# Down projection of a SwiGLU block as seven block products instead of eight, on one Trainium2 core

## The chip, the cores and the metric

The kernel runs on one core of a Trainium2 chip. The metric is the device time of one execution in microseconds (us). TensorE (PE in the profile, its weight loads PEld) multiplies matrices, VectorE (DVE), ScalarE (ACT) and GpSimd (POOL) do elementwise work, SyncE (SP) issues most of the DMAs.

## The reference

A trunk of two layers on 1024 tokens of width 1024 in float32: an mLSTM mixer, then chunked attention, each followed by a SwiGLU feed-forward block with hidden width 2816, and a final RMSNorm. What the change touches:

```python
def swiglu(h, w_gate, w_up, w_down):
    return (jax.nn.silu(h @ w_gate) * (h @ w_up)) @ w_down

# per layer
h = h + swiglu(rmsnorm(h, norm_ffn_g[l]), ffn_w_gate[l], ffn_w_up[l], ffn_w_down[l])
# after the last layer
return rmsnorm(h, final_norm_g)
```

## The kernel before

Everything is kept transposed: features on the 128 partitions, tokens along the row. A feature tile is 128 features by 1024 tokens (a half: 512 tokens), so the residual `h` is 8 tiles and the hidden layer 22. For float32 accuracy each operand is split into a rounded part and a remainder (`split_into`: ScalarE copies the rounded part, VectorE subtracts), and each block of a product takes three matmuls: high by high, low by high, high by low.

The gate and up projections (`gate_up`) already work by 2x2 blocks in seven products, as in the method of Strassen and Winograd. Feature tiles p and p+11 and the two token halves make the blocks. A unit is one pair of tiles of one of the two matrices; there are 22 units, worked one after the other, and each has products c = 0 to 6 of 12 matmuls of 512 columns. `prepare` makes the seven weight sums of a unit and their splits (`wc`), seven products ahead. The operand sums come from `Mixed`: `mix` makes those of products 0 to 3 while the mixer's output projection is running, `late` those of products 4 to 6 (`b21`, `t4`, `b22`), which the first unit calls for between its own products. `st.finish` turns the sums of squares into the norm's factors `f_rbc` after product 3 of the first unit. `add` also stores `h` to DRAM (`hd`). `gate` and `up` finish each half tile, and `up` stores the hidden tile to DRAM (`hid`).

The down projection (`ffn`) multiplies the plain way. The 22 hidden tiles are cut into four blocks of 4, 6, 6 and 6 tiles (`PBLOCKS`). For each block `fetch` loads the hidden tiles and splits them, and for each of the 8 output tiles and both halves the block's matmuls run (tile `d_p`) and VectorE adds the result to `h` (L1073). Weights come through `Weights`, one tile ahead. In layer 0 the last block also makes the statistics and the operands of attention (`finalize_mid`), in layer 1 it works by columns 0 to 511, 512 to 767 and 768 to 1023 (`PIECES`, tile `dl`), and normalises, scales and stores each piece as soon as it is whole (`finalize_last`).

Instructions are traced in the order of the code; a scheduler then sets each engine's queue, and an instruction may go ahead of earlier ones when its data and its buffers are free. A tile waits until the tiles that lay in its memory have been used for the last time. The pool `core` has 25 tiles of 128 x 1024; in `gate_up` 24 of them hold the operand sums.

Of the kernel before, what the change touches and what calls it, by code (L numbers as in the profile page):

```python
# [8 lines left out]
F32 = mybir.dt.float32  # L9
F32R = mybir.dt.float32r  # L10
# [7 lines left out]
NK = 8  # L18
# [7 lines left out]
PBLOCKS = (2, 3, 3, 3)  # L26
# [7 lines left out]
PIECES = ((0, 512), (512, 256), (768, 256))  # L34
# [7 lines left out]
def tile_trunk(  # L42
# [80 lines left out]
    class Weights:  # L123
# [9 lines left out]
        def add(self, key, src, n=T, g=None, pool=None):  # L133
            self.specs.append((key, src if isinstance(src, list) else [src], n, g, pool))
# [52 lines left out]

    def feat_cols(w, xs, ps, cols):

        whi, wlo = w  # L190
        n = len(xs)
        for k in range(n):
            wh = whi[:, k * P : (k + 1) * P]
            wl = wlo[:, k * P : (k + 1) * P]
            xh, xl = (a[:, cols] for a in xs[k])
            for i, (a, b) in enumerate(((wh, xh), (wl, xh), (wh, xl))):
                nc.tensor.matmul(  # L197
                    ps, a, b, start=(k == 0 and i == 0), stop=(k == n - 1 and i == 2)
                )
            yield 3  # L200
# [16 lines left out]
    def tok_proj(wv, xs, name, evac):  # L217

        for c in range(T // P):
            pv = pjt(f"{name}_{c}")  # L220
            for k in range(NK):
                wh, wl = (w[:, (k % 4) * 256 : (k % 4 + 1) * 256] for w in wv[k // 4])
                xh, xl = (a[:, c * P : (c + 1) * P] for a in xs[k])
                for i, (a, w) in enumerate(((xh, wh), (xh, wl), (xl, wh))):
                    nc.tensor.matmul(  # L225
                        pv[:, 0:256], a, w, start=(k == 0 and i == 0), stop=(k == 7 and i == 2)
                    )
                if k % 2:
                    yield 3
            evac(c, pv)  # L230
# [118 lines left out]
    def down_weights(layer):  # L349
        p0 = 0  # L350
        for b, nb in enumerate(PBLOCKS):
            last = layer == 1 and b == len(PBLOCKS) - 1
            for e in range(NK):
                src = [
                    w_down[layer, e][:, (p0 + d) * P : (p0 + d + nb) * P] for d in (0, NP)
                ]
                wts.add(("d", layer, b, e), src, 2 * nb * P, pool="core" if last else None)
            p0 += nb

    wts.fence()  # L360
    down_weights(0)
# [10 lines left out]
    wts.fence()  # L372
    down_weights(1)
# [467 lines left out]
    class Mixed:  # L841
# [60 lines left out]
    def gate_up(layer, mixed, st):  # L902
# [24 lines left out]
        def prepare(m):  # L927

            n, c = divmod(m, NC)
# [16 lines left out]
            t = full("hl", f"wc{layer}{m}", F32R)  # L946
# [3 lines left out]
            ready[m] = t  # L950

        at = [0]

        def product(n, c, ps, name, first):
            m = n * NC + c
            ahead = AHEAD if n else min(AHEAD, 2 + c)
            while at[0] < min(m + 1 + ahead, NC * len(units)):
                prepare(at[0])
                at[0] += 1
            w = ready.pop(m)  # L960
# [26 lines left out]

        def up(f, h, x, ps=None):
# [5 lines left out]
            if f not in hid:  # L994
                hid[f] = dram.tile([P, T], F32, tag=f"f{layer}{f}", name=f"hid{layer}{f}")
            nc.sync.dma_start(hid[f][:, hs(h)], x)

        for n, (p, i) in enumerate(units):
# [10 lines left out]
            if n == 0:  # L1009
                mixed.late(0)  # L1010
                mixed.late(1)
# [4 lines left out]
            if n == 0:  # L1016
                mixed.late(2)
                mixed.late(3)
# [3 lines left out]
            tt(c22, c, v, ALU.add)  # L1022
            d = pjt(f"d{layer}{n}")
# [4 lines left out]
            done(p + NP, 1, c22)  # L1028
            product(n, 4, a, "b21", False)
            done(p, 0, tmp("c11"), a)  # L1030
            product(n, 5, c, "t4", False)
            c21 = tmp("c21")
            tt(c21, c, v, ALU.add)
            done(p + NP, 0, c21)
            product(n, 6, d, "b22", False)
            tt(v, v, d, ALU.subtract)
            done(p, 1, v)
        sb.close()
# [3 lines left out]
    def ffn(layer, mixed, st, finalize):  # L1042
        psc = Scope(mx=2, pj=6)
        kept = gate_up(layer, mixed, st)
        wsc = wscope()
        sb = Scope(half=6, hr=2, ex=16)
        pairs = iter(range(NP))
        blocks = []
        for nb in PBLOCKS:
            ps_ = [next(pairs) for _ in range(nb)]  # L1050
            blocks.append(ps_ + [p + NP for p in ps_])

        def fetch(b, f):
            raw = full("hr" if b else "core", f"hr{layer}{f}")
            nc.sync.dma_start(raw, kept[f])
            return split(raw, f"hid{layer}{f}", pool="ex" if b % 2 else "core")

        hid = [fetch(0, f) for f in blocks[0]]
# [5 lines left out]
        for b, fs in enumerate(blocks):  # L1064
            if b == len(blocks) - 1:
                finalize(layer, b, h, hid)
                break
            nxt = []
            for e in range(NK):

                def ed(hh, ps):
                    s_ = h[e][:, hs(hh)]
                    nc.vector.tensor_tensor(s_, s_, ps, ALU.add)  # L1073

                run(feat(wts.get("d", layer, b, e), hid, f"d{layer}{b}{e}", ed))
                if len(nxt) < len(blocks[b + 1]):
                    nxt.append(fetch(b + 1, blocks[b + 1][len(nxt)]))
            hid = nxt
        psc.close()
        sb.close()  # L1080
        return wsc

    def finalize_mid(layer, b, h, hid):
        st = Stats("b")
        for e in range(NK):

            def ed(hh, ps):
                s_ = h[e][:, hs(hh)]
                nc.vector.tensor_tensor(s_, s_, ps, ALU.add)
                st.add(s_, hs(hh))  # L1090

            run(feat(wts.get("d", layer, b, e), hid, f"d{layer}{b}{e}", ed))
            xb.append(split(h[e], f"xb{e}"))
        stb.append(st)

    def finalize_last(layer, b, h, hid):
        st = Stats("fin")
        ws = [wts.get("d", layer, b, e) for e in range(NK)]
        r_bc = ext("fin_rbc")
        for c0, n in PIECES:  # L1100
            cols = slice(c0, c0 + n)
            for e in range(NK):
                ps = pjt(f"dl{c0}_{e}")[:, 0:n]
                run(feat_cols(ws[e], hid, ps, cols))
                s_ = h[e][:, cols]
                nc.vector.tensor_tensor(s_, s_, ps, ALU.add)
                st.add(s_, cols)
            st.finish(r_bc, cols)
            for e in range(NK):
                s_ = h[e][:, cols]  # L1110
                if e % 3 == 0:
                    nc.scalar.activation(s_, s_, AF.Copy, scale=gcol(G_FIN, e))
                    nc.gpsimd.tensor_tensor(s_, s_, r_bc[:, cols], ALU.mult)
                else:
                    nc.vector.scalar_tensor_tensor(
                        s_, s_, gcol(G_FIN, e), r_bc[:, cols], ALU.mult, ALU.mult
                    )
                (nc.sync if e % 2 else nc.scalar).dma_start(out[e][:, cols], s_)
# [235 lines left out]
    xb, stb = [], []  # L1354
    mixed, st = mlstm()
    wsc = ffn(0, mixed, st, finalize_mid)
    mixed, st = attention(xb, stb[0])
    wsc.close()
    ffn(1, mixed, st, finalize_last).close()
# [92 lines left out]
```

## Time and profile before

| | |
|---|---|
| Median of 3 runs | 2458.86 us (2457.55 to 2460.49) |
| Profiled execution, its own time | 2460.18 us |
| Its span | 2458.4 us |
| PE busy | 2383.3 us, 97% of the span |
| Mean granted TensorE clock | 0.989 of full |

A busy share says how long an engine had an instruction in work; overlapping instructions count once. Waits are put down to what came last before the waiting instruction started. The profiled execution is one run: 1.3 us above the median.

### The profile page before, as it was taken

Reading aid. Unit: us, or ns where it says so; the run is one execution under the profiler, and the core shown is the slowest. Engines: PE = TensorE matmul, PEld = TensorE weight load, DVE = VectorE, ACT = ScalarE, POOL = GpSimd, SP = SyncE. Lnnn points to the kernel's source line nnn. Section 1 sums busy time; section 2 is a strip of 40 time slices with the busy share of each in tenths; the row PEclk is TensorE's granted clock in tenths of the full one; section 3 lists DMA queues with packets and bytes.
Section 4 is the critical chain, followed back from the end, with each engine's and each line's share of the span. In section 5 each row is a group of like instructions: output and inputs, shape, how many; then the busy total and the mean of one; then the engine's idle time right before and its main releaser. Section 6 shows DMA issues by size and latency. Waiting matters only on the chain.

```text
span 2458.4 us, 31074 instructions
## 1 busy us (share of the span) xinstructions
PE 2383.3 (97%) x11844; PEld 1973.6 (80%) x11844; DVE 1508.8 (61%) x2451; ACT 890.7 (36%) x1592; POOL 887.3 (36%) x582
## 2 busy tenths in 40 slices
PE   8999999889999999999999999989899999999998
PEld 7888787768888888888879788878678888888887
DVE  6544446886666655334377777787976666645334
ACT  5322222543232333113366666655532233323122
POOL 2000000476455540003564545350865655530003
PEclk9999999989999999999999999999999999999999
DMA  3110102312222217211111111001222222145211
GB/s 134 44 35 26 43 29 75 134 68 82 94 85 80 83 59 261 88 60 52 49 44 44 37 37 41 30 23 48 107 78 103 78 78 86 69 160 192 62 58 69
DMA packets 74885, 185.85 MB, mean 76 GB/s; under 512 B 8304, under 2 KB 26992, under 8 KB 74736
## 3 DMA queue, kind: packets, MB, share of 16 engines
q1 hardware_dynamic: 73008, 181.76, 21.9%
q8 instruction: 93, 1.52, 0.3%
q10 hardware_dynamic: 1728, 2.10, 0.2%
q14 instruction: 56, 0.46, 0.1%
HBM read 148.18 MB, written 35.65 MB: 75 GB/s over the span
## 4 chain that ended last, share of the span: by engine, by line
PE 87%; DVE 7%; ACT 3%; issue 1%; POOL 1%; DMA 0%; SPq 0%; DVEq 0%; ACTq 0%; POOLq 0%
PE d_p L197 17%; PE d L966 10%; PE c L966 9%; PE a L966 9%; PE b L966 5%; PE pv L225 4%; PE ao_p L197 4%; PE pvb L225 4%; PE bq_p L197 2%; PE bk_p L197 2%; PE dl L197 2%; PE wa_p L197 2%; PE wb_p L197 2%; PE ak_p L197 2%; PE ob_p L197 2%; PE po L1272 2%
## 5 line engine op out<-in xcount | busy, mean ns | idle before, releaser
L966 PE MATMUL a<-b,wc 128*128 128x512 f32 x1056 | 265.9, 400 | 21.9 <-ACT wc L947 11.0
L966 PEld LDWEIGHTS a<-b,wc 128*128 128x128 f32 x1056 | 202.5, 193 | 70.1 <-ACT wc L947 11.8
L966 PE MATMUL c<-t,wc 128*128 128x512 f32 x1056 | 258.1, 394 | 0.0
L966 PEld LDWEIGHTS c<-t,wc 128*128 128x128 f32 x1056 | 199.9, 189 | 44.1 <-ACT wc L947 0.3
L949 DVE TENSOR_TENSOR wc<-s,wc 128x512 fp32r<-128x512 f32 x168 | 158.3, 944 | 94.2 <-ACT wc L947 92.3
L947 ACT CAST wc<-s 128x512 fp32r<-128x512 f32 x176 | 108.2, 619 | 216.7 <-PE d L966 127.9
L1073 DVE TENSOR_TENSOR hr<-hr,d_p 128x512 f32<-128x512 f32 x96 | 65.8, 686 | 162.1 <-PE d_p L197 161.9
L727 POOL TENSOR_TENSOR hv<-num 128x1024 f32<-128x1024 f32 x8 | 15.2, 1895 | 342.5 <-ACT num L703 342.5
L161 ACT CAST wh_d<-wr_d 128x768 fp32r<-128x768 f32 (+1 forms) x64 | 49.8, 781 | 241.2 <-PE d_p L197 223.8
L981 POOL TENSOR_TENSOR c<-c,f_rbc 128x512 f32<-128x512 f32 x44 | 75.1, 1707 | 157.4 <-DVE c L1027 150.0
L966 PE MATMUL d<-b,wc 128*128 128x512 f32 x528 | 131.1, 397 | 0.8 <-DVE c L1027 0.8
L966 PE MATMUL b<-t,wc 128*128 128x512 f32 x528 | 128.7, 393 | 3.0 <-POOL wc L949 1.8
L947 ACT CAST wc<-wr 128x512 fp32r<-128x512 f32 x132 | 81.1, 618 | 135.3 <-PE a L966 42.3
L966 PE MATMUL d<-n,wc 128*128 128x512 f32 x528 | 128.0, 391 | 0.0
L966 PEld LDWEIGHTS b<-t,wc 128*128 128x128 f32 x528 | 99.3, 188 | 25.7 <-POOL wc L949 2.5
L966 PEld LDWEIGHTS d<-b,wc 128*128 128x128 f32 x528 | 99.3, 188 | 25.2 <-DVE c L1027 1.2
L1232 ACT ACTIVATE p<-p,mn 128x640 f32<-128x640 f32 (+4 forms) x128 | 89.2, 697 | 83.6 <-DVE mn L1221 77.0
L966 PEld LDWEIGHTS d<-n,wc 128*128 128x128 f32 x528 | 99.2, 188 | 21.7
L991 POOL TENSOR_TENSOR c<-c,c 128x512 f32<-128x512 f32 x44 | 74.3, 1689 | 106.2 <-issue 69.2
L1236 DVE TENSOR_SCALAR p<-p,rs 128x640 f32<-128x640 f32 (+4 forms) x128 | 109.1, 852 | 2.9
L949 DVE TENSOR_TENSOR wc<-wr,wc 128x512 fp32r<-128x512 f32 x126 | 106.2, 843 | 6.1 <-ACT wc L947 5.7
L985 POOL TENSOR_TENSOR c<-c,f_rbc 128x512 f32<-128x512 f32 x66 | 94.5, 1434 | 30.3 <-ACT c L984 28.8
(1146 smaller groups left out, 6561.0 us busy)
## 6 DMA issues: line engine op xcount, KB each, us to landing
wr<-in_w_gate_dram SPq DMA_DIRECT2D x44, 512.0 KB, 4.3
wr<-in_w_up_dram SPq DMA_DIRECT2D x44, 512.0 KB, 4.3
hr<-hid SPq DMA_DIRECT2D x44, 512.0 KB, 3.7
wr_d<-in_w_down_dram SPq DMA_DIRECT2D x96, 192.0 KB, 2.5
hid<-c SPq DMA_DIRECT2D x66, 256.0 KB, 2.4
hd<-h SPq DMA_DIRECT2D x16, 512.0 KB, 2.7
hr<-hd SPq DMA_DIRECT2D x16, 512.0 KB, 6.0
hid<-v SPq DMA_DIRECT2D x22, 256.0 KB, 2.0
```

What stands on the lines that cost most here:

```text
L161: nc.scalar.copy(hi[:, :n], raw[:, :n])
L197: nc.tensor.matmul(ps, a, b, start=(k == 0 and i == 0), stop=(k == n - 1 and i == 2))
L225: nc.tensor.matmul(pv[:, 0:256], a, w, start=(k == 0 and i == 0), stop=(k == 7 and i == 2))
L947: nc.scalar.copy(t[:, 0:HT], src)
L949: eng.tensor_tensor(t[:, HT:T], src, t[:, 0:HT], ALU.subtract)
L966: nc.tensor.matmul(ps, a, b, start=(first and k == 0 and i == 0), stop=(k == len(xs) - 1 and i == 2), skip_group_check=True,)
L981: nc.gpsimd.tensor_tensor(x, x, r, ALU.mult)
L985: nc.gpsimd.tensor_tensor(x, x, r, ALU.mult)
L991: nc.gpsimd.tensor_tensor(x, x, g, ALU.mult)
L1073: nc.vector.tensor_tensor(s_, s_, ps, ALU.add)
L1232: nc.scalar.activation(p, p, AF.Exp, bias=mnv, scale=-1.0, accum_out=sm)
L1236: eng.tensor_scalar(p, p, rs, None, ALU.mult)
```

## The change

The down projection of both layers is done by 2x2 blocks in seven products as well: output tiles u and u+4, hidden tiles p and p+11, and the two token halves. Product by product, for each u = 0 to 3, one PSUM bank sums 11 feature tiles x 3 matmuls. `up` now makes the operand sums `n1`, `t2`, `t3`, `t4` per pair and stores seven half tiles instead of two whole ones. `fetch` brings one product's 11 half tiles into `core`; `combine` makes the weight sums in place in the raw weights; `settle` adds each product into the residual. In `gate_up` the first two units are interleaved: products 0 to 3 of both, then 4 to 6 of both, with one `late` after each of the first four products. Half of the stores of `h` move from `add` to `late`. The first weights of attention are no longer behind the down weights in one list, and matmuls with 8 operands take tiles 4 to 7 first in layer 1. The last norm is done by two halves. The core of the diff:

```diff
-PBLOCKS = (2, 3, 3, 3)
+WC = NP * P
-PIECES = ((0, 512), (512, 256), (768, 256))
-        def add(self, e, h):
+        def keep(self, e, h):
             kept = dram.tile([P, T], F32, tag=f"h{self.layer}{e}", name=f"hd{self.layer}{e}")
             nc.sync.dma_start(kept, h)
             self.kept[e] = kept
+        def add(self, e, h):
+            if e < NK // 2:
+                self.keep(e, h)
...
         def late(self, k):
             h2, t2 = self.got.pop(k)
             e = k + NK // 2
+            self.keep(e, h2)
...
+        order = [(n, c) for cs in (range(4), range(4, NC)) for n in range(2) for c in cs]
+        order += [(n, c) for n in range(2, len(units)) for c in range(NC)]
...
+            i, p = divmod(f, NP)
+            part[i, h] = x
+            if (i, h) != (0, 1):
+                store(f"b{i + 1}{h + 1}", p, x)
+                return
+            n1, t2, t3, t4 = (halft(f"{nm}{layer}_{p}") for nm in ("n1", "t2", "t3", "t4"))
+            nc.gpsimd.tensor_tensor(t3, part[1, 1], x, ALU.subtract)
+            store("t3", p, t3)
+            nc.vector.tensor_tensor(n1, part[0, 0], x, ALU.subtract)
+            store("n1", p, n1)
+            nc.vector.tensor_tensor(t2, part[1, 1], n1, ALU.add)
+            store("t2", p, t2)
+            nc.gpsimd.tensor_tensor(t4, part[1, 0], t2, ALU.subtract)
+            store("t4", p, t4)
...
+        first, second = unit(0), unit(1)
+        for k in range(4):
+            next(first)
+            mixed.late(k)
+        for _ in range(4):
+            next(second)
+        for u in (first, second):
+            for _ in u:
+                pass
...
+    def down(layer, mixed, hid):
+        sb = Scope(hr=6, half=8, wc=2, wd=12)
+        names = ("b11", "t2", "n1", "t4", "t3", "b21", "b22")
+        NU = NK // 2
+        pieces = [(c, min(HT, WC - c)) for c in range(0, WC, HT)]
...
+        def fetch(i, k):
+            r = hrt(f"hr{layer}{i}_{k}")
+            nc.sync.dma_start(r, hid[names[i], k])
+            t = coret(f"hc{layer}{i}_{k}", F32R)
+            split_into(t[:, 0:HT], t[:, HT:T], r)
+            sums[i, k] = t
+        def combine(i, u):
+            a11, a21, a22 = raw[u, 0, 0], raw[u, 1, 0], raw[u, 1, 1]
+            if i == 1:
+                nc.gpsimd.tensor_tensor(a21, a11, a21, ALU.subtract)
+                nc.vector.tensor_tensor(a21, a22, a21, ALU.subtract)
+            if i == 2:
+                nc.gpsimd.tensor_tensor(a11, a21, a11, ALU.add)
+            if i == 4:
+                nc.vector.tensor_tensor(a22, a22, a21, ALU.subtract)
+            if i == 6:
+                a12 = raw[u, 0, 1]
+                nc.gpsimd.tensor_tensor(a12, a21, a12, ALU.subtract)
+        def prepare(i, u):
+            t = pools["wc"].tile([P, 2, WC], F32R, tag="wc", name=f"wc{layer}{i}{u}")
...
+                split_into(t[:, 0, c : c + n], t[:, 1, c : c + n], src)
+            if i == 2:
+                wload(u, 0, 1)
...
+        def settle(i, u, ps):
...
+            if i == 0:
+                v[u] = halft(f"v{layer}{u}")
+                nc.scalar.copy(v[u], ps)
+                tt(r11, r11, ps, ALU.add)
+            if i == 1:
+                tt(v[u], v[u], ps, ALU.add)
+                for r in (r12, r21, r22):
+                    nc.gpsimd.tensor_tensor(r, r, v[u], ALU.add)
+            if i == 2:
+                tt(r22, r22, ps, ALU.subtract)
+                tt(r12, r12, ps, ALU.subtract)
+            if i in (3, 4):
+                tt(r21, r21, ps, ALU.add)
...
+        prepare(0, 0)
+        for k in range(NP):
+            fetch(0, k)
+        for u in range(NU):
+            wload(u, 0, 0)
         for e in range(NK):
             ht = coret(f"hr{layer}_{e}")
             nc.sync.dma_start(ht, mixed.kept[e])
             h.append(ht)
+        for u in range(NU):
+            wload(u, 1, 0)
+            wload(u, 1, 1)
+        order = [(i, u) for i in range(len(names)) for u in range(NU)]
+        for m, (i, u) in enumerate(order):
+            if m + 2 < len(order):
+                combine(*order[m + 2])
+            if m + 1 < len(order):
+                prepare(*order[m + 1])
+            w = wcs.pop((i, u))
+            ps = pjt(f"dn{layer}{i}{u}")
+            for k in range(NP):
+                wh, wl = (w[:, j, k * P : (k + 1) * P] for j in range(2))
+                x = sums[i, k]
+                xh, xl = x[:, 0:HT], x[:, HT:T]
+                for j, (a, b) in enumerate(((wh, xh), (wl, xh), (wh, xl))):
+                    nc.tensor.matmul(
+                        ps, a, b, start=(k == 0 and j == 0), stop=(k == NP - 1 and j == 2)
+                    )
+            if i + 1 < len(names):
+                for k in (range(0, 2), range(2, 4), range(4, 5), range(5, NP))[u]:
+                    fetch(i + 1, k)
+            settle(i, u, ps)
+            if last and i >= 5 and u == NU - 1:
+                if i == 5:
+                    r_fin.append(coret("fin_rbc"))
+                scale_out(i - 5)
```

## Rows read from the trace of the kernel before

**Rows 1.** Page, busy time of each engine, and the chain that ended last.
```profile
PE 2383.3 (97%) x11844; PEld 1973.6 (80%) x11844; DVE 1508.8 (61%) x2451; ACT 890.7 (36%) x1592; POOL 887.3 (36%) x582
PE 87%; DVE 7%; ACT 3%; issue 1%; POOL 1%; DMA 0%; SPq 0%; DVEq 0%; ACTq 0%; POOLq 0%
```
**Rows 2.** Busy time by stretch (start:end, length, then as the header says).
```profile
core 0: us, PE busy (x) PEld busy (x) DVE busy (x) ACT busy (x) POOL busy (x), PEclk, DMA share, GB/s
532.00:917.00 385.00, 385.00 (x1678) 314.96 (x1677) 249.90 (x297) 118.13 (x203) 220.78 (x143) 1.00 0.23 80
...
934.00:990.00 56.00, 56.00 (x247) 46.03 (x246) 32.97 (x40) 20.01 (x23) 1.49 (x2) 1.00 0.79 269
```
**Rows 3.** Chain in order of time, down projections (start us, us, what).
```profile
933.86 240.54 PE d_p L197 x1056
...
2199.05 175.20 PE d_p L197 x768
2374.25 33.60 PE dl L197 x144
...
2432.51 13.09 PE dl L197 x111
```
**Rows 4.** Timeline of PE, first units of gate and up, layer 0, then layer 1.
```profile
490.90 0.80 PE L966 MATMUL a<-b,wc 128*128 128x512 f32 x1 [6.36 <-ACT wc L947]
506.24 1.84 PE L309 MATMUL f_ps<-ones,f_s 128*128 128x1 f32 x16
513.37 0.50 PE L966 MATMUL a<-b,wc 128*128 128x512 f32 x1 [3.34 <-DVE b L179]
516.46 1.97 PE L966 MATMUL a<-b,wc 128*128 128x512 f32 x3 [2.59 <-ACT b L178]
531.16 2.91 PE L966 MATMUL b<-t,wc 128*128 128x512 f32 x12
...
1770.94 1.84 PE L309 MATMUL f_ps<-ones,f_s 128*128 128x1 f32 x16
1791.47 3.41 PE L321 MATMUL f_pb<-packed,f_y 128*128 128x128 f32 x16 [2.40 <-DVE f_y L278]
1796.36 2.91 PE L966 MATMUL b<-t,wc 128*128 128x512 f32 x12
```
**Rows 5.** Timeline of DVE in the same stretch of layer 0.
```profile
499.67 3.50 DVE L895 SCALAR_TENSOR_TENSOR t<-h,packed,t 128x512 f32<-128x512 f32 x2
...
516.18 1.40 DVE L179 SCALAR_TENSOR_TENSOR b<-h,packed,b 128x512 fp32r<-128x512 f32 x2
```
**Rows 6.** Durations by line: min/median/max ns, first and last start.
```profile
L949 DVE TENSOR_TENSOR wc<-s,wc x168: 675/694/1787, 517.5 to 2172.2; 128x512 fp32r<-128x512 f32 x168
L949 POOL TENSOR_TENSOR wc<-s,wc x8: 1280/1734/1754, 496.7 to 1776.5; 128x512 fp32r<-128x512 f32 x8
L163 POOL TENSOR_TENSOR wl_bq<-wr_bq,wh_bq x8: 2365/2388/2411, 1167.5 to 1569.7; 128x1024 fp32r<-128x1024 f32 x8
L176 DVE TENSOR_TENSOR hid01l<-hr,hid01h x1: 1225/1225/1225, 921.3 to 921.3; 128x1024 fp32r<-128x1024 f32 x1
L1073 DVE TENSOR_TENSOR hr<-hr,d_p x96: 678/687/690, 936.7 to 2374.3; 128x512 f32<-128x512 f32 x96
```
**Rows 7.** Busy time by stretch around the first down projection's start.
```profile
925.00:935.00 10.00, 10.00 (x45) 8.17 (x44) 4.93 (x6) 2.10 (x2) 2.88 (x3) 1.00 0.62 199
935.00:945.00 10.00, 10.00 (x46) 8.20 (x45) 2.87 (x5) 0.69 (x2) 1.01 (x1) 1.00 0.97 376
```
**Rows 8.** DMA issues: count, KB each, median us to landing.
```profile
hid<-c SPq DMA_DIRECT2D x66, 256.0 KB, 2.4
hr<-hd SPq DMA_DIRECT2D x16, 512.0 KB, 6.0
```
**Rows 9.** Chain at the end, after the first piece of 512 columns.
```profile
2414.00 1.11 PE fin_pb L321 x8
...
2415.76 6.59 DVE hr L1115 x5
```

More of the change, by code (lines that the diff above doesn't have):

```diff
@@ L185, in split, with k_order @@
         return hi, lo
+    second_first = [False]
+    def k_order(n):
+        if second_first[0] and n == NK:
+            return list(range(NK // 2, NK)) + list(range(NK // 2))
+        return list(range(n))
     def feat_cols(w, xs, ps, cols):
@@ L191, in feat_cols @@
         n = len(xs)
-        for k in range(n):
+        for at, k in enumerate(k_order(n)):
             wh = whi[:, k * P : (k + 1) * P]
@@ L197, in feat_cols @@
                 nc.tensor.matmul(
-                    ps, a, b, start=(k == 0 and i == 0), stop=(k == n - 1 and i == 2)
+                    ps, a, b, start=(at == 0 and i == 0), stop=(at == n - 1 and i == 2)
                 )
@@ L220, in tok_proj @@
             pv = pjt(f"{name}_{c}")
-            for k in range(NK):
+            for at, k in enumerate(k_order(NK)):
                 wh, wl = (w[:, (k % 4) * 256 : (k % 4 + 1) * 256] for w in wv[k // 4])
@@ L225, in tok_proj @@
                     nc.tensor.matmul(
-                        pv[:, 0:256], a, w, start=(k == 0 and i == 0), stop=(k == 7 and i == 2)
+                        pv[:, 0:256], a, w, start=(at == 0 and i == 0), stop=(at == 7 and i == 2)
                     )
@@ L347, in tile_trunk @@
         wts.add(("wb", e), w_aout[e][:, KA * P : T], T - KA * P)
[L349 to L358, printed above, removed]
     wts.fence()
-    down_weights(0)
     for t in range(8):
@@ L945, in prepare @@
             src = (a11, s2, s3, s1, a12, a22, s4)[c]
-            t = full("hl", f"wc{layer}{m}", F32R)
+            t = full("hl", f"wc{layer}{n}_{c}", F32R)
             nc.scalar.copy(t[:, 0:HT], src)
@@ L986, in gate, with store @@
             gs[f, h] = x
+        def store(name, p, x):
+            t = dram.tile([P, HT], F32, tag=f"{name}_{layer}{p}", name=f"k{name}_{layer}{p}")
+            nc.sync.dma_start(t, x)
+            hid[name, p] = t
+        part = {}
         def up(f, h, x, ps=None):
@@ L993, in up, with unit @@
                 nc.vector.tensor_tensor(x, ps, g, ALU.mult)
[L994 to L998, printed above, removed]
+            i, p = divmod(f, NP)
[12 more added lines that the diff above has]
+            store("t4", p, t4)
+        def unit(n):
+            p, i = units[n]
             done = (gate, up)[i]
@@ L1037, in gate_up @@
             done(p, 1, v)
+            yield
+        first, second = unit(0), unit(1)
[7 more added lines that the diff above has]
+                pass
+        for n in range(2, len(units)):
+            for _ in unit(n):
+                pass
         sb.close()
@@ L1063, in ffn @@
             h.append(ht)
[L1064 to L1078, printed above, removed]
@@ L1079, in ffn @@
-        psc.close()
[L1080 to L1118, printed above, removed]
@@ L1121, in attention, with ffn @@
+        sb.close()
+        return xs, st
+    def ffn(layer, mixed, st):
+        psc = Scope(mx=1, pj=7)
+        kept = gate_up(layer, mixed, st)
+        psc.close()
+        psc = Scope(mx=2, pj=6)
+        res = down(layer, mixed, kept)
+        psc.close()
+        return res
     def attention(xs, st):
@@ L1352, in attention @@
         return mixed, st
[L1354 removed]
     mixed, st = mlstm()
[L1356 to L1357 removed]
+    xb, st = ffn(0, mixed, st)
+    wsc = wscope()
+    second_first[0] = True
+    mixed, st = attention(xb, st)
     wsc.close()
[L1359 removed]
+    ffn(1, mixed, st)
     base.close()
```

99 lines of the change are left out of this document (70 added, 29 removed).

## Prediction

> **What bounds the kernel now.** I read the page first: TensorE is busy 97% of the span, and the chain that ended last runs 87% over it [rows 1]. That is a share of a whole; what a stage is worth has to be read in the stage. So next the busy times by stretch: in the steady part of gate and up, and in the first 56 us of the down projection, TensorE has no idle time at the full granted clock, VectorE is at 65% and 59% [rows 2]. The chain in order of time says the same: 1056 matmuls of the down projection in layer 0 follow one another in 240.54 us [rows 3], so one costs 240.54 / 1056 = 0.2278 us there. In these stages a matmul less is 0.2278 us less, as long as what feeds it keeps up. Last I read the two places where TensorE does stand: the first units of gate and up in both layers [rows 4] and the tail, 2458.4 - 2445.6 = 12.8 us after the last matmul (2432.51 + 13.09) [rows 3].
>
> **Matmuls.** Before: 8 output tiles x 2 halves x 22 hidden tiles x 3 = 1056 per layer. After: 7 products x 4 x 11 x 3 = 924, of the same shape and with a new weight for each, as before. Two layers: 264 x 0.2278 = -60.1 us.
>
> **The end of layer 1.** Before, from the first to the last matmul 2445.60 - 2199.05 = 246.5 us for work that at 0.2278 us takes 240.5: 6 us went to statistics and to waits between the three pieces. After there is one such break (4 row sums, then `fin_pb` of 1.11 us [rows 9]) in product 6: -3, between 0 and -5. The tail, however, now handles 512 columns instead of 256. Five scalings of 512 columns took 6.59 us [rows 9], so half of that, 3.3, is added there, and about 1.7 in the add, the square, the sum and a larger last store: +5, between 3.3 and 12.8 (all of it doubled). Together +2.
>
> **First units interleaved.** Layer 0: from the end of product 3 (506.24) to the second product of unit 1 (531.16) [rows 4] are 24.9 us, for four products of 12 x 0.2278 = 2.73 us, 1.84 us of row sums and, I take it, as much for the factors' matmuls `f_pb`: some 10.3 us are lost. Waits of 3.34 and 2.59 us for `late`'s splits are in it. Layer 1: 1770.94 to 1796.36 are 25.4 us, with 3.41 for `f_pb` some 9.2 are lost. The reason is VectorE, which works on `late` from 499.67 to 517.58 [rows 5]. Interleaved, four products of unit 1 (11 us) go in front of the first that needs `late`. But they want three more weight splits early (at up to 1.79 us each [rows 6], some 5 us), so VectorE ends `late` near 523 instead of 517.6, while TensorE asks at 506.24 + 1.84 + 11 = 519. I take 6 of 10 us as won, in two layers -12; the bounds are 0 (unit 1's weights late instead) and -20 (all of it). The wait of 6.36 us ahead of the first product stays: nothing there is taken away but stores of `h` that move behind it, which I count at nothing.
>
> **Start of the down projection.** Until product 1 starts, 4 x 33 x 0.2278 = 30.1 us in, these must land: 11 half tiles (2.9 MB), the first weights twice for one tile and once for three (3.6 MB), `h` (4.2 MB), the other eight weight halves (5.8 MB), five half tiles of product 1 (1.3 MB): 17.7 MB. The DMAs moved 199 GB/s in the 10 us around the boundary and 376 when 97% busy [rows 7]. 30.1 us at 376 are 11.3 MB; the other 6.4 MB have to come in the 20 us before, in which the weight tiles and the operands of products 0 to 2 of the last unit fall free. At 199 that is 4.0 MB, 2.4 short, 6.4 us late; at 376 nothing is late. I take +3 per layer, bounds 0 and 6.4.
>
> **The port of VectorE and GpSimd.** A subtraction of 512 columns with both inputs in SBUF takes VectorE 0.69 us, but up to 1.79; GpSimd takes 1.28 alone and 1.73 in the median [rows 6]. Additions that read PSUM keep to 0.68 to 0.69 throughout. So the first kind hardly overlaps with GpSimd: 0.69 + 1.28 = 1.97 us of work in 1.79. By columns, a weight half of 1408 takes VectorE 1.225 x 1.375 = 1.7 us and GpSimd 2.39 x 1.375 = 3.3 us. In products 1 and 2 (60.2 us) GpSimd has 6 combines (19.7) and 12 additions of `settle` (15.4); VectorE has 2 combines (3.4), 8 weight splits (8 x 2.75 x 0.694 = 15.3) and 22 operand splits (15.3). That is 69 us one after the other, or 63 at the overlap seen; 12 additions from PSUM (8.3) also stand in VectorE's queue. The 12 GpSimd additions may slip into product 3, where GpSimd has no other work, so the loss can be nothing; at most it is 69.1 + 8.3 - 60.2 = 17. Nearer the lower end, since six PSUM banks let the additions wait: +5 per layer. With the start that is +8 per layer, +16.
> The Trainium skill's page SBUF — State Buffer, section Who interferes with whom, says that a VectorE instruction with two SBUF inputs and a GpSimd instruction that reads SBUF use one port in turn, the second fully blocked. The rows above agree nearly (1.79 of 1.97), and by the rule alone this term would be 8.9 instead of 5, the whole some 8 us more.
>
> **Between products.** `core` has 25 tiles: 8 of `h`, one of statistics, 11 operands, so 5 of the next product can be early. The other six wait until the last unit's matmuls free a tile each 3 x 0.2278 = 0.68 us, the first 6.8 us before the boundary; it is wanted as the sixth, 3.4 us behind it. That leaves 10.2 us for a landing (2.4 us for 256 KB [rows 8]) and two splits of at most 1.8: hidden with over 4 us to spare. Without that cover it would be paid at 12 boundaries.
>
> **Into attention.** The first attention weights were loaded behind the last down weights; now their memory is that of `hr` and `half`, of which `hr` is free a whole product early. If none came early, a 512 KB landing (6.0 [rows 8]) and two GpSimd passes of 2.4 would be open, 11 us. I take +1.5, bounds 0 and 11. The residual's last tile is used as the last of eight operands, 21 matmuls (4.8 us) in; its addition, square and split take about that.
>
> **Gate and up in the steady part.** Per pair two more VectorE and two more GpSimd operations: in a layer 22 x 0.69 to 1.79 = 15 to 39 us on VectorE, 22 x 1.75 = 39 on GpSimd. Over 385 us they have 250 and 221 busy [rows 2], so both stay under 80% and TensorE's work covers them: nothing. The three more stores per pair, 8.7 MB a layer, go into a DMA share of 0.23.
>
> **Sum.** -60.1 + 2 - 12 + 16 + 1.5 = -52.6 us. From the profiled execution's 2460.18 that is 2407.6; the median of the runs lies 1.3 lower. I say 2407.
>
> **Rivals.** First, everything new is hidden: loads start early enough, GpSimd's additions slip, and interleaving wins its whole 20. -60.1 + 2 - 20 = -78, 2382. For it: in the old down projection GpSimd was busy 1.49 us of 56 and VectorE 33 [rows 2], so there is room; against it: 69 us of port work in 60. Second, the port and the loads take their upper bounds: (17 + 6.4) x 2 instead of 16 is 31 more, 2438. For it: VectorE runs its queue in order, so a weight split waits behind a blocked combine. Third, the other side: the operands between products are late. With only five tiles early, each of 12 boundaries stalls by what the chain from a freed tile to its split takes beyond 10.2 us. It ends slower than before if that is over 10.2 + 52.6 / 12 = 14.6 us; at 16.5 the 12 stalls cost 76, 2483. Against it stands the 6 us chain above; for it, that `fetch`, the weight splits and the combines share two queues in order, and 512 KB loads in the full stretch took 6.0 us in the median.
>
> **Chances.** The forecast 0.67 (its own range 2394 to 2420: interleaving worth nothing is 12 more, either start term at nothing 6 to 10 less), the first rival 0.14, the second 0.12, the third 0.05; 0.02 for a mixture that comes out even. Faster by over 0.2% (5 us, about what a measurement of this kernel can tell from no change) are the first three: 0.93; within it 0.02, slower 0.05. The range 2384 to 2434 leaves out half of each of the first two rivals and the third, some 0.2.
>
> **What would show it.** 924 matmuls per layer at 0.228 us, about 210.5 us if fed. Where the feed fails, an idle TensorE ahead of the first or second unit of product 1, released by VectorE (port) or a DMA (start); at the first matmuls of later products for the third rival. In the first units, no wait for `b21` and `b22`, perhaps one for `wc` of unit 1. A tail near 18 us. The prediction is wrong if TensorE's pace differs in runs of 33 matmuls into one bank, if GpSimd's additions hold up VectorE in products 2 and 3, or if gate and up show idle time in the steady part.

## The result, and the profile after

The changed kernel takes 2486.95 us (median of four runs, 2485.57 to 2492.88), the kernel before 2458.37 beside it: 1.0122 of the time before, 95% interval 1.0110 to 1.0134. Forecast were 2407 and a range up to 2434: wrong in size and in sign. The profiled execution of the changed kernel has a span of 2489.9 us, 31.5 more than before; it is the slowest of the four, 5.9 us above their median.

I first cut both traces at the first matmul of each stage. The rows are profiled executions, but for the second, which is the first with the prediction's terms added; the last three are experiments told further down. Each number is the difference of two start times of matmuls in the timeline of PE (down 1 and the tail: to the end of the down projection's last matmul, and from there to the span's end). Each row is a single execution, and the four of the changed kernel lie within 7.3 us of each other, so a difference of a few us between two rows says little.

| us | to gate/up 0 | gate/up 0 | down 0 | to gate/up 1 | gate/up 1 | down 1 | tail | span |
|---|---|---|---|---|---|---|---|---|
| before | 490.9 | 442.8 | 240.5 | 579.3 | 445.3 | 246.7 | 12.8 | 2458.4 |
| forecast | 490.9 | 436.8 | 218.5 | 580.8 | 439.3 | 221.6 | 17.8 | 2405.8 |
| changed | 491.2 | 446.3 | 253.7 | 580.1 | 446.2 | 253.5 | 19.0 | 2489.9 |
| sums on VectorE | 488.0 | 447.0 | 235.5 | 578.6 | 445.7 | 233.7 | 19.0 | 2447.4 |
| and early tiles | 489.3 | 445.9 | 227.6 | 581.7 | 445.7 | 227.2 | 19.0 | 2436.4 |
| and units in turn | 489.9 | 443.3 | 226.5 | 581.4 | 445.9 | 227.3 | 19.8 | 2434.1 |

Of the 84.1 us between the forecast and the execution, 35.2 lie in the down projection of layer 0, 31.9 in that of layer 1 and 16.4 in the two gate and up stages. Some 3.5 of the 35.2 belong to the way into attention, as told at the end. The waits of PE name the places (us in total, times, longest):

```profile
PE dn L1218 <- ACT wc L174: 25.9, 4, 10.4
PE dn L1218 <- DVE hc L175: 22.5, 4, 9.3
PE f_pb L328 <- DVE f_y L285: 19.7, 2, 10.6
PE a L966 <- ACT wc L944: 11.0, 2, 6.4
PE dn L1218 <- DVE wc L175: 9.1, 5, 2.7
```

The fourth stood before too (6.36 in [rows 4]); the others are new or far longer. Next, where the three on `dn` stand: timeline of PE at the start of the first down projection, the idle time ahead of each piece in brackets.

```profile
938.96 7.62 PE L1218 MATMUL dn<-hc,wc 128*128 128x512 f32 x32 [1.15 <-DVE wc L175]
957.02 28.21 PE L1218 MATMUL dn<-hc,wc 128*128 128x512 f32 x108 [10.43 <-ACT wc L174]
988.65 0.50 PE L1218 MATMUL dn<-hc,wc 128*128 128x512 f32 x1 [3.42 <-ACT wc L174]
991.84 4.64 PE L1218 MATMUL dn<-hc,wc 128*128 128x512 f32 x10 [2.69 <-DVE wc L175]
1005.81 1.65 PE L1218 MATMUL dn<-hc,wc 128*128 128x512 f32 x3 [9.33 <-DVE hc L175]
1009.38 6.97 PE L1218 MATMUL dn<-hc,wc 128*128 128x512 f32 x20 [1.93 <-DVE hc L175]
```

There are two places. After the 33 matmuls of the first unit, PE waits 10.43 us for weights; in product 1, the second of the seven, it waits 17.4 us in four pieces for splits. Layer 1 has the same six waits (1.16, 8.39, 3.61, 2.69, 9.35, 1.93). Windows of the changed kernel (columns as in [rows 2]) show what the machine does in them:

```profile
500.00:520.00 20.00, 17.77 (x86) 14.56 (x84) 20.00 (x20) 13.19 (x23) 15.98 (x10) 1.00 0.16 54
946.00:968.00 22.00, 11.57 (x38) 8.66 (x37) 4.21 (x7) 3.92 (x8) 0.00 (x0) 0.69 1.01 399
988.00:1002.00 14.00, 5.14 (x11) 3.36 (x11) 9.24 (x5) 4.65 (x9) 11.71 (x4) 0.70 0.00 0
1002.00:1012.00 10.00, 4.26 (x9) 2.96 (x10) 8.48 (x8) 0.62 (x1) 4.97 (x2) 0.50 0.22 74
1040.00:1160.00 120.00, 120.00 (x526) 98.45 (x525) 94.02 (x120) 54.19 (x102) 25.34 (x12) 1.00 0.34 110
1860.00:2200.00 340.00, 339.95 (x1480) 277.40 (x1479) 248.16 (x283) 102.64 (x178) 221.03 (x141) 1.00 0.29 104
```

From 946 to 968 the DMA engines are the full ones, and VectorE and GpSimd have nearly nothing to do: the first place is a late load. From 988 to 1002 no byte moves and GpSimd works 11.71 of 14 us: the second place is not a load. In the later products (1040 to 1160) PE never stops, and 120.00 / 526 = 0.2281 us a matmul is the forecast's pace.

**The first place.** Timeline of the SP queue, where loads are issued:

```profile
943.40 2.08 SPq L990 DMA_DIRECT2D kt<-t  x2
945.59 0.88 SPq L1200 DMA_DIRECT2D hr<-hd  x2
946.52 3.31 SPq L1097 DMA_DIRECT2D wd<-in_w_down_dram  x4
```

The down weights are issued 9 us after the stage has begun (937.42), behind the last stores of gate and up, and with 704 KB each they take 10.9 us to land, in the median over all 32 of the kernel.

**The second place.** Timelines of DVE, then of POOL, in product 1. L1113 on DVE and L1112 and L1115 on POOL are the weight sums of `combine`; L175 is the low part of a split.

```profile
979.05 7.30 DVE L175 TENSOR_TENSOR wc<-wd,wc 128x512 fp32r<-128x512 f32 x3 [0.74 <-ACT wc L174]
988.63 6.74 DVE L175 TENSOR_TENSOR wc<-wd,wc 128x512 fp32r<-128x512 f32 x2
1003.52 1.63 DVE L1113 TENSOR_TENSOR wd<-wd,wd 128x1408 f32<-128x1408 f32 x1 [6.14 <-POOL wd L1112]
1005.07 7.27 DVE L175 TENSOR_TENSOR hc<-hr,hc 128x512 fp32r<-128x512 f32 x7
```

```profile
981.65 3.69 POOL L1112 TENSOR_TENSOR wd<-wd,wd 128x1408 f32<-128x1408 f32 x1
988.06 3.17 POOL L1115 TENSOR_TENSOR wd<-wd,wd 128x1408 f32<-128x1408 f32 x1 [2.72 <-DVE wd L1113]
991.19 3.63 POOL L1112 TENSOR_TENSOR wd<-wd,wd 128x1408 f32<-128x1408 f32 x1
```

Three splits that alone take 0.68 or 0.54 us take 7.30 together, two take 6.74. The durations of the line over the whole kernel (min/median/max ns) have the same end:

```profile
L175 DVE TENSOR_TENSOR wc<-wd,wc x162: 543/685/3723, 957.0 to 2458.6; 128x512 fp32r<-128x512 f32 x108, 128x384 fp32r<-128x384 f32 x54
```

The longest, 3723 ns, is 3.0 us over the median, about the length of one GpSimd sum (3.1 to 3.7). And at 1003.52 a sum on VectorE waits 6.14 us for one on GpSimd, while the seven operand splits for which PE stands since 996.5 are queued behind it. Two explanations offer themselves here, the shared port and the order in VectorE's queue; experiments have to part them.

**The first units.** Timeline of PE, then of DVE, in layer 0:

```profile
507.33 1.84 PE L316 MATMUL f_ps<-ones,f_s 128*128 128x1 f32 x16
528.41 2.05 PE L328 MATMUL f_pb<-packed,f_y 128*128 128x128 f32 x8 [10.63 <-DVE f_y L285]
```

```profile
517.77 0.15 DVE L322 TENSOR_SCALAR f_v<-f_ps 128x8 f32<-128x8 f32 x1
527.01 1.25 DVE L285 SCALAR_TENSOR_TENSOR f_y<-f_t,f_y 128x8 f32<-128x8 f32 x1
```

The waits for `late` of [rows 4] (3.34 and 2.59) are gone. In their place PE waits 10.63 us for the row factors: the row sums are done at 509.2, VectorE reaches them at 517.77 and, between splits, needs until 528.3 for a dozen small steps. The kernel before had the same limit. A window of it (VectorE is the third pair of numbers), then its timeline of PE:

```profile
500.00:520.00 20.00, 14.07 (x61) 10.76 (x61) 20.00 (x20) 10.46 (x18) 17.23 (x11) 0.88 0.16 54
```

```profile
527.43 2.05 PE L321 MATMUL f_pb<-packed,f_y 128*128 128x128 f32 x16 [0.72 <-DVE f_y L278]
```

VectorE had no idle time there either, and the factors came at 527.4, 1 us earlier than now. So the products moved ahead bring TensorE sooner to a result that comes no sooner.

### The profile page after: what moved, and what is told of

It reads as the page before. It is cut to its first block, busy times and chain, and to the rows that moved or that the text cites. A ratio compares the mean times of both kernels' runs of the same rounds, so it can differ in the third digit from the quotient of the medians.

```text
span 2489.9 us, 30852 instructions
## 1 busy us (share of the span) xinstructions
PE 2340.5 (94%) x11436; PEld 1925.8 (77%) x11436; DVE 1733.1 (70%) x2642; ACT 966.3 (39%) x1802; POOL 1092.9 (44%) x666
## 5 line engine op out<-in xcount | busy, mean ns | idle before, releaser
L1218 PE MATMUL dn<-hc,wc 128*128 128x512 f32 x1848 | 442.8, 402 | 57.6 <-ACT wc L174 25.9
L1218 PEld LDWEIGHTS dn<-hc,wc 128*128 128x128 f32 x1848 | 355.5, 193 | 143.7 <-ACT wc L174 27.6
L946 DVE TENSOR_TENSOR wc<-s,wc 128x512 fp32r<-128x512 f32 x168 | 182.0, 1085 | 71.2 <-ACT wc L944 70.4
L175 DVE TENSOR_TENSOR wc<-wd,wc 128x512 fp32r<-128x512 f32 x162 | 164.8, 1062 | 12.8 <-ACT wc L174 12.2
L174 ACT CAST wc<-wd 128x512 fp32r<-128x512 f32 x162 | 85.8, 580 | 157.7 <-PE dn L1218 101.5
L175 DVE TENSOR_TENSOR hc<-hr,hc 128x512 fp32r<-128x512 f32 x154 | 127.5, 878 | 21.2 <-ACT hc L174 21.0
L946 DVE TENSOR_TENSOR wc<-wr,wc 128x512 fp32r<-128x512 f32 x126 | 115.9, 920 | 17.4 <-ACT wc L944 17.3
L174 ACT CAST hc<-hr 128x512 fp32r<-128x512 f32 x154 | 87.1, 618 | 96.0 <-DMA hr<-kt 54.0
## 6 DMA issues: line engine op xcount, KB each, us to landing
wd<-in_w_down_dram SPq DMA_DIRECT2D x32, 704.0 KB, 10.9
```

The lines of the kernel that those rows point to most:

```text
L174: nc.scalar.copy(hi, src)
L175: nc.vector.tensor_tensor(lo, src, hi, ALU.subtract)
L946: eng.tensor_tensor(t[:, HT:T], src, t[:, 0:HT], ALU.subtract)
L1218: nc.tensor.matmul(ps, a, b, start=(k == 0 and j == 0), stop=(k == NP - 1 and j == 2))
```

## The experiments

Times on different chips are compared by their ratio to the kernel before on the same chip.

**Units in turn.** The interleaving undone, the new down projection kept:
```diff
-        order = [(n, c) for cs in (range(4), range(4, NC)) for n in range(2) for c in cs]
-        order += [(n, c) for n in range(2, len(units)) for c in range(NC)]
+        order = [(n, c) for n in range(len(units)) for c in range(NC)]
...
-        for k in range(4):
-            next(first)
-            mixed.late(k)
-        for _ in range(4):
-            next(second)
+        for k in range(2):
+            next(first)
+            mixed.late(2 * k)
+            mixed.late(2 * k + 1)
```


> The interleaving of the first two units is undone, the down projection stays new. Theory A (the interleaving won nothing, because the matmuls that spread the norm's factors stand in TensorE's queue ahead of a product that doesn't need them, and wait 10.6 and 9.1 us there for VectorE, which was as late before): 2483 to 2491 us, and the waits for the operands of products 4 to 6 come back in their place. Theory B (the interleaving is worth its 6 us per layer as predicted and only the down projection lost): 2497 to 2501 us.

Measured 2482.36 us, 1.0106 (1.0087 to 1.0124), 0.16% below the changed kernel, with about 0.2% of uncertainty on that difference. No gain from the interleaving is seen, and the slowdown lies elsewhere.

**Sums on VectorE.** The three GpSimd lines of `combine` moved:
```diff
-                nc.gpsimd.tensor_tensor(a21, a11, a21, ALU.subtract)
+                nc.vector.tensor_tensor(a21, a11, a21, ALU.subtract)
...
-                nc.gpsimd.tensor_tensor(a11, a21, a11, ALU.add)
+                nc.vector.tensor_tensor(a11, a21, a11, ALU.add)
...
-                nc.gpsimd.tensor_tensor(a12, a21, a12, ALU.subtract)
+                nc.vector.tensor_tensor(a12, a21, a12, ALU.subtract)
```


> The weight sums of the down projection, of which GpSimd makes three in four passes, are all made by VectorE. Theory A (the passes of 3.3 us on GpSimd hold the port, so that splits of 0.69 us beside them take 2.4 to 3.7 us, and VectorE's queue stands behind them): a sum of 1408 columns costs VectorE 1.6 us, the stall at the start of product 1 falls from 17 to about 6 us per layer and the time to 2460 to 2470 us. Theory B (the stall is set by when weights and operands land): 2484 to 2490 us.

Measured 2452.14 us, 0.9983 (0.9973 to 0.9992): 34 us below the changed kernel (1.0122 - 0.9983 = 1.39%), better than expected. VectorE makes 24 more sums of 1.62 us (39 us of work), and yet is sooner done. The same line of durations, then PE's timeline at the first place:

```profile
L175 DVE TENSOR_TENSOR wc<-wd,wc x162: 543/684/1795, 953.0 to 2416.1; 128x512 fp32r<-128x512 f32 x108, 128x384 fp32r<-128x384 f32 x54
```

```profile
953.06 27.52 PE L1218 MATMUL dn<-hc,wc 128*128 128x512 f32 x109 [8.95 <-ACT wc L174]
987.54 25.72 PE L1218 MATMUL dn<-hc,wc 128*128 128x512 f32 x111 [1.71 <-DVE hc L175]
```

No split takes longer than 1.8 us now, and the wait of 9.33 on `hc` is 1.71. The late first weights stay.

**No sums.** `combine` is not called; the products take the unsummed blocks.
```diff
-            if m + 2 < len(order):
-                combine(*order[m + 2])
```


> The weight sums of the down projection are left out (the raw blocks are used in their place), all loads, splits and matmuls stay. Theory A (weight sums on the port and in VectorE's queue make the stall at product 1): the 17 us and what the clock loses behind them go, 2440 to 2452 us. Theory B (operands land late, behind the second half of the weights in the DMA queue): the stall stays at 10 us or more per layer, 2475 us or more.

Measured 2438.42 us, 0.9927 (0.9911 to 0.9943). So on GpSimd and VectorE the sums cost 1.95%, 48 us, and on VectorE alone still 0.56%, 14 us.

**Weights early.** The first halves for units 1 to 3 get tiles of their own, which gate and up's end doesn't use, and ACT's queue issues them. Not shown: `wc` becomes two pools of one tile, and these loads come ahead of the operand loads in the code.
```diff
-        sb = Scope(hr=6, half=8, wc=2, wd=12)
+        sb = Scope(hr=6, half=8, wc0=1, wa=3, wc1=1, wd=9)
...
-            t = pools["wd"].tile([P, WC], F32, tag="wd", name=f"wd{layer}{u}{i}{j}")
-            nc.sync.dma_start(t, wsrc(u, i, j))
+            pool = "wa" if i == 0 and u > 0 else "wd"
+            t = pools[pool].tile([P, WC], F32, tag=pool, name=f"wd{layer}{u}{i}{j}")
+            (nc.scalar if (i, j) == (0, 0) and u else nc.sync).dma_start(t, wsrc(u, i, j))
...
```


> The three first weight halves of product 0 get memory that gate and up free early and are issued from ScalarE's queue, so that they no longer stand behind the last stores of gate and up; the rest stays. The wait of 10.4 and 8.4 us after the first unit should go in either case. Theory A (the burst of weight sums ends when it ends, about 72 us after the start, because it begins when the second half of the weights lands): what is won at the start is lost again in product 1, 2479 to 2487 us. Theory B (the waits add up): 2460 to 2470 us.

Measured 2480.27 us, 1.0095 (1.0079 to 1.0111). In place of the wait of 10.43 us for weights stands one of 2.79 for operands, but product 1 stands as before:

```profile
948.64 25.21 PE L1221 MATMUL dn<-hc,wc 128*128 128x512 f32 x102 [2.79 <-ACT hc L174]
1001.07 1.65 PE L1221 MATMUL dn<-hc,wc 128*128 128x512 f32 x3 [8.88 <-DVE hc L175]
```

The waits of PE on `dn` in layer 0 fall from 29.0 to 20.8 us. The time falls by 0.27% (1.0122 to 1.0095), 7 us, with about 0.2% of uncertainty.

**Factors late.** The matmuls that spread the row factors move from unit 1's fourth product to behind the ninth; the `gate` and `up` that need the factors wait for them in a list (not shown: `st.finish` returns these matmuls as a function, pinned to their place in the code):
```diff
-                st.finish(r_bc, pin=True)
+                late.append(st.finish(r_bc, pin=True))
...
             tt(c22, c22, d, ALU.subtract)
-            done(p + NP, 1, c22)
+            if n < 2:
+                late.append(lambda: done(p + NP, 1, c22))
+            else:
+                done(p + NP, 1, c22)
             yield
             product(n, 4, a, "b21", False)
+            while late:
+                late.pop(0)()
```


> Only the first two units of a layer change: the eight small matmuls that spread the row factors (f_pb) stand behind product 4 of unit 0, the ninth product, and no longer inside unit 1's product 3; the gate of unit 0's first part and the up of unit 1's first part move behind them. Theory A (the wait of f_pb on f_y, 10.6 and 9.1 us, is why interleaving won nothing): both waits go, nothing takes their place, 2464 to 2473 us, about 1.003 to 1.006 of the kernel before. Theory B (the first units are held back by weight sums and VectorE's queue whatever stands in TensorE's): another wait of 6 us or more stands in each of the two places, 2480 to 2489 us.

Measured 2488.46 us, 1.0126 (1.0109 to 1.0143): nothing won. The wait on `f_y` fell from 19.7 to 8.7 us, and 5.2 of a new one came, 2.6 in layer 0 in the next unit and 2.6 in layer 1:

```profile
PE f_pb L330 <- DVE f_y L285: 8.7, 2, 4.5
PE c L974 <- DVE c L1048: 5.2, 3, 2.6
```

So the place in TensorE's queue is not the cause; what VectorE has not done is waited for somewhere else.

**Sums on GpSimd.** To part port and queue order, all sums away from VectorE:
```diff
-                nc.vector.tensor_tensor(a21, a22, a21, ALU.subtract)
+                nc.gpsimd.tensor_tensor(a21, a22, a21, ALU.subtract)
...
-                nc.vector.tensor_tensor(a22, a22, a21, ALU.subtract)
+                nc.gpsimd.tensor_tensor(a22, a22, a21, ALU.subtract)
```


> All weight sums of the down projection on GpSimd (the eight that VectorE makes go there too), everything else as in the changed kernel. Theory 'queue order' (the operand splits hc are late because they stand in VectorE's queue behind sums that wait for GpSimd): the waits on hc, 22.5 us in all, go to under 8, and the kernel takes 2462 to 2474 us. Theory 'shared port' (they are late because every split beside a GpSimd sum of 3.1 to 3.7 us takes 2.4 to 3.7 us in place of 0.6): GpSimd now works longer in one piece, the splits beside it stay as long, the waits on hc and wc stay at 35 us or more in all, and the kernel takes 2480 to 2500 us.

Measured 2498.73 us, 1.0166 (1.0149 to 1.0183), 0.44%, 11 us, above the changed kernel. No sum stands in VectorE's queue any more, but the waits of PE on `hc` are 22.3 us after 22.5, and the splits in product 1 take longer still. Timelines of DVE, then of POOL:

```profile
979.97 10.15 DVE L175 TENSOR_TENSOR wc<-wd,wc 128x512 fp32r<-128x512 f32 x3
990.64 10.07 DVE L175 TENSOR_TENSOR wc<-wd,wc 128x512 fp32r<-128x512 f32 x3
1000.64 13.79 DVE L175 TENSOR_TENSOR hc<-hr,hc 128x512 fp32r<-128x512 f32 x8
```

```profile
982.60 3.53 POOL L1113 TENSOR_TENSOR wd<-wd,wd 128x1408 f32<-128x1408 f32 x1
986.20 3.50 POOL L1115 TENSOR_TENSOR wd<-wd,wd 128x1408 f32<-128x1408 f32 x1
```

Beside an unbroken row of GpSimd sums of 3.5 us, three splits take 10.15: one split for each sum. That is what a shared port would do; the order of a queue makes no single split longer. The sum in VectorE's queue at 1003.52 made one wait of it, but is not its cause. What this run leaves open: the operand splits still stand behind six weight splits (979.97 to 1000.7) in VectorE's queue, and no run put them ahead.

**Both edits of the down projection.** Sums on VectorE and early tiles, as in the two diffs above.

> Both edits of the down projection together: all weight sums on VectorE, and the first halves of the weights of units 1 to 3 of a layer in tiles of their own whose loads go out early. With the sums on VectorE alone the time was 2452 us, with early loads alone 2480 (6.7 below the changed kernel). Theory A (early loads were worth little only because the next product stood at the sums): the wait of 9.0 and 8.5 us on the first weights goes and comes back nowhere, 2434 to 2441 us. Theory B (what is won at the start is lost again in product 1, where the second halves of the weights have to land anyway): 2447 to 2453 us.

Measured 2438.90 us, 0.9929 (0.9912 to 0.9946). The first unit and the three behind it now run in one piece, but for 1.15 us behind the first matmul:

```profile
936.65 30.77 PE L1221 MATMUL dn<-hc,wc 128*128 128x512 f32 x131 [1.15 <-DVE wc L175]
972.04 37.71 PE L1221 MATMUL dn<-hc,wc 128*128 128x512 f32 x151 [2.59 <-DVE wc L175]
```

The early loads, worth 0.27% alone, are worth 0.54%, 13 us, here (0.9983 to 0.9929). With about 0.2% of uncertainty on each, the runs do not tell the two apart, and PE's waits on `dn` in layer 0 fall by 8 us in both cases (here from 15.9 to 7.9).

**All three.** The same with the factors late.

> The three edits together: weight sums on VectorE, early tiles for the first halves of the weights, and the row factors' matmuls behind the ninth product. If the three causes are separate places that only add up, the time is 2452 less 13 to 17 at the first weights and less 15 to 19 at the row factors: 2416 to 2426 us, 0.983 to 0.987 of the kernel before. If the places share one limit (VectorE's queue, or the loads), 2432 us or more.

Measured 2437.34 us, 0.9919 (0.9904 to 0.9934), within its interval equal to the run before: the third edit again adds nothing.

**Both edits, units in turn.** The two down edits with the first diff of this section.

> As the version with all weight sums on VectorE and early tiles for the first halves of the weights (0.9929 of the kernel before), with the first two units of a layer in turn again in place of interleaved. Theory A (interleaving moved waits about and won nothing, as in the run with the units in turn alone): 2430 to 2441 us, within 0.3% of that version, f_pb waits under 5 us in all. Theory B (interleaving does win once TensorE is not held back elsewhere): 2445 to 2453 us.

Measured 2435.89 us, 0.9906 (0.9889 to 0.9922): the lowest time of a version with the whole computation, within its interval equal to the two runs before, and it has no interleaving.

**VectorE busier.** In `late`, ahead of each `t4`:
```diff
+            for _ in range(2):
+                nc.vector.tensor_tensor(t4, h2[:, 0:HT], t2, ALU.add)
```


> The changed kernel with eight more VectorE additions of 128x512 in each layer, two ahead of each t4 of the late operands of the mixed input (their result is written over by the t4 that follows, so the output is unchanged). Theory A (in the first two units VectorE is the bound, 20.00 of 20 us busy from 500 to 520, and the interleaved products only wait for it in another place): every added addition, 0.68 us alone and up to 1.8 beside GpSimd, appears whole in the wait of f_pb on f_y: 5 to 13 us more in each layer, 2497 to 2513 us. Theory B (the wait is one of order in TensorE's queue, and VectorE has room): under 3 us more in all, 2484 to 2490 us.

Measured 2500.61 us, 1.0163 (1.0147 to 1.0178): 0.41%, 10 us, above the changed kernel, which speaks for a full VectorE. But the wait on `f_y` did not grow (17.5 us), against theory A's place for it: cut by matmuls, the two gate and up stages are 448.7 and 451.8 us, 2.4 and 5.6 longer, spread over several waits; the remainder I did not find.

**No sums, weights early.** The third and fourth diff together, the sums left out again.

> The weight sums of the down projection left out (its products take the unsummed blocks, so the output is not the reference's), with the early tiles for the first halves of the weights. It shows what the down projection takes without both causes. Theory A (the two causes, late first weights and weight sums, are all that held it back): the wait on first weights goes as it did with the sums on VectorE, and the time is 13 to 17 us below the 2438 us with the sums left out alone: 2421 to 2427 us. Theory B (a third cause is behind them, such as the time the operands of the second product take to arrive): 2431 to 2438 us.

Measured 2430.74 us, 0.9885 (0.9870 to 0.9900), between the two theories. With both causes away, a third stands behind them: 3.65 us at operands of product 1.

```profile
978.15 32.83 PE L1219 MATMUL dn<-hc,wc 128*128 128x512 f32 x136 [3.65 <-ACT hc L174]
```

**Interleaving alone.** In the kernel before, only the order of the first units (and in that stage PSUM as 7 and 1 banks, as in the change); the edit is the `order`, `unit` and `next` lines of the change's own diff.

> The kernel before with one part of the change alone: its first two gate and up units of a layer interleaved (first four products of each, then the rest of each), the down projection as it was. Theory A (VectorE's queue in that stretch is the bound, so the waits that interleaving removes, 6 us and 4 us ahead of the first products, come back whole at the row factors): 2455 to 2466 us, no faster than before, with f_pb waits of 9 us or more in each layer. Theory B (the prediction's step: 12 us won by interleaving, and the changed down projection spoils it): 2440 to 2450 us.

Measured 2459.25 us, 1.0005 (0.9995 to 1.0015): nothing, without any change of the down projection. Waits of PE around layer 0's first units, then a window of the same run:

```profile
PE f_pb L321 <- DVE f_y L278: 8.9, 1, 8.9
```

```profile
500.00:520.00 20.00, 17.57 (x85) 14.38 (x84) 20.00 (x24) 12.12 (x22) 15.21 (x10) 1.00 0.16 54
```

In layer 1 the wait on `f_y` is 4.5 us, half of what theory A had named; there too VectorE is busy for all of the 20 us around `late` (1766 to 1786).

## Why the prediction was wrong

**Matmuls (-60.1): right.** `dn` has 1848 matmuls, 0.2281 us each where they are fed. What was wrong is the feed at the start.

**The port of VectorE and GpSimd (+5 per layer, at most 17): the step that failed most.** The durations were right: 3.3 us forecast for a GpSimd sum, 3.1 to 3.7 measured; 1.7 for one on VectorE, 1.62 measured. The arithmetic on them was not. I added 69 us of port work up, set it against the 60 us of products 1 and 2, and let the surplus slip. But eight sums on GpSimd and four on VectorE (not six and two) fall into the 40 us from 969 to 1009, as the second halves of the weights land and just when product 1 wants its weights and operands. And beside these sums the unit of loss is not the split's own time but one whole GpSimd sum for each split. The waits in product 1 are 17.4 and 17.6 us, just above the upper bound, before the clock is counted. Against no sums at all the step cost 48 us in two layers, not 10; 34 of them went when VectorE alone made the sums.
The Trainium skill's page SBUF — State Buffer, section Who interferes with whom, whose rule of an exclusive lock I weighed there, describes the trace (10.15 us for three splits beside 3.5 us sums); taken as a sum of work over 60 us, as I took it, it gave 8.9 and would have failed too.

**Start of the down projection (+3 per layer, at most 6.4): failed.** I counted bytes against the 20 us before the boundary and took for granted that they could be issued there. The first `wd` load goes out 9 us behind the boundary. Ahead of it in SP's queue stand the last unit's stores, which wait there for its results; whether the tiles' memory was free by then is not shown. The wait was 10.43 and 8.39 us. With tiles of their own, another queue and an earlier place in the code for these loads (and the sums on VectorE), PE runs 131 matmuls without a break; which of the three would do alone was not tried.

**First units interleaved (-12): failed.** The waits on `late` did go, but gate and up took 3.5 and 0.9 us more than before in the profiled executions. The step's fault is that it treated VectorE's 18 us of `late` as a delay that other products can cover, while VectorE is full there, before the change as after it (20.00 of 20 us), and the row factors, which it makes in the same queue, are wanted next. The interleaving alone moved the time by nothing. I had named a wait for `wc` as a possible new one; it was `f_y`.

**Not in the sum: the clock.** Behind the long waits TensorE is granted less. From 1002 to 1012 it is 0.50, the lower of its two levels (1.2 GHz), after 5.14 us of work in the 14 before. In the timeline of PE above, the 108, 10, 3 and 20 matmuls behind waits take 28.21, 4.64, 1.65 and 6.97 us for 24.6, 2.3, 0.7 and 4.6 at full pace: 9.3 us more in layer 0, a third on top of its 29 us of waits.

**Into attention (+1.5): too small, within its bounds.** I had counted the residual's last tile and the weights, but not the row sums, which now stand between the last down matmul and attention's first and before stood at 1185.7, inside attention. Timeline of PE:

```profile
1187.65 0.95 PE L316 MATMUL b_ps<-ones,b_s 128*128 128x1 f32 x8
1189.97 1.05 PE L316 MATMUL b_ps<-ones,b_s 128*128 128x1 f32 x8 [1.38 <-DVE b_s L309]
1194.63 0.79 PE L204 MATMUL bk_p<-xb4h,wl_bk 128*128 128x512 f32 x1 [1.76 <-POOL wl_bk L162]
```

From 1187.65 to gate and up of layer 1 are 583.6 us, against 579.3 before: 4.3 more. In the table above, 3.5 of them are in down 0.

**Right:** the tail (near 18 forecast, 19.0 measured); the break at the end of layer 1 (3 us left for it; a wait of 1.98 us and 2 us of small matmuls stand there); between products (no stall in layer 0 from 1011 to the end of its down projection, and in layer 1 one of 1.44 us, inside product 5; this refutes the third rival, the one that stood for a slower kernel); gate and up in the steady part (339.95 of 340 us busy in layer 1). The first rival is refuted too. The second had the right mechanism, port and loads, and a price of 2438: its upper bounds were averages over too long a stretch, and it kept the interleaving's 12 us and left out the clock. The sign went wrong in the down projections: by the table they are 67.1 us above the forecast, more than the 52.6 that were to be won.

**What stays open:** of the 60.1 us that the matmuls give, the best version keeps some 23. Its down projections still take 226.5 and 227.3 us for 210.5 of matmuls, the tail takes 7.0 more than before; the row sums ahead of attention (3.5 us in layer 0), waits for weight splits (2.6 us at most) and the arrival of operands are part of it. No run tried to spread the loads of the second halves.

## What to carry to other kernels

Price a burst against the stretch in which it must be done, not against the stage it belongs to: list what becomes ready at one moment, what the next matmul needs of it, and what stands ahead of that in each queue. Here a large elementwise pass on GpSimd beside short ones on VectorE, both with two SBUF inputs, cost VectorE one whole pass for each short instruction, and the large passes were better made on VectorE although it got more work. Before a transfer is called hidden, find the first moment at which it can be issued (whose memory its tile takes, what stands before it in the queue); and before products are moved ahead of a wait, see whether the engine that is waited for has any idle time at all.

## What was not expected of the hardware

A VectorE subtraction of 128x512 took up to 3.72 us beside GpSimd's 128x1408 sums (0.68 alone, at most 1.79 beside the 512-column operations of [rows 6]). Handing 39 us of sums to VectorE made the kernel 34 us faster. And the loads, at 399 GB/s from 946 to 968, were above the 376 GB/s taken from [rows 7].
